# One stored table of cosines and sines per batch, read twice, with the sign taken in the scan

## The chip, the cores and the metric

The kernel runs on one core of a Trainium2 chip. The core has a matrix engine (TensorE, in the profile PE, with its weight loads as PEld), a vector engine (VectorE, DVE), a scalar engine (ScalarE, ACT), a general engine (GpSimd, POOL) and an engine that issues transfers (SyncE, SP). Transfers run on the core's 16 DMA engines. The metric is device time of one execution in microseconds (us).

## The reference

One layer of a decoder with x of 1024 rows and 1024 columns, in float32:

```python
h = modulate(rms_norm(x, ffn1_norm), sh1, sc1)
x = x + 0.5 * g1 * swiglu(h, ffn1_w_gate, ffn1_w_up, ffn1_w_down)

h = modulate(rms_norm(x, mix_norm), sh2, sc2)
b_gate, c_gate, v, u = split(h @ w_in, [512, 1024, 1536])
y_conv = b_gate * causal_conv3(c_gate * v, conv_w)
y_ssm = s5_mixer(u, ...)
y_mix = concat([rms_norm(y_conv, out_norm_conv), rms_norm(y_ssm, out_norm_ssm)])
x = x + g2 * (y_mix @ w_out)

h = modulate(rms_norm(x, ffn2_norm), sh3, sc3)
x = x + 0.5 * g3 * swiglu(h, ffn2_w_gate, ffn2_w_up, ffn2_w_down)
return rms_norm(x, final_norm)
```

The part that the change touches is `s5_mixer`, a diagonal state space model of 32 groups, each with 16 channels and 64 complex states:

```python
lam_bar = exp(lam * dt)                       # a complex factor per group and state
bu      = einsum('gpc,bsgc->bsgp', b_bar, u)  # inputs of the states
state_t = lam_bar * state_(t-1) + bu_t        # over the 1024 rows
y       = Re(einsum('gcp,bsgp->bsgc', c, state)) + d_skip * u
y       = gelu(y);  y = y * sigmoid(y @ glu_w + glu_b)
```

## The kernel before, in words

The large products (two feed-forward networks of 2816 inner columns, the input projection, the output projection, the gate matrix) are cut into products of 128 by 128 by 512 on TensorE; most go through a seven-product scheme (`seven`), which forms sums of blocks on DVE and ACT and spares one product in eight. Weights are streamed: SP loads a raw chunk of 128 by 1024, POOL's queue may add a second one to it in memory (line 175), DVE and ACT turn it into the operands `w`. Three raw chunks may be held at a time. Side work is cut into steps by generators and put between the steps of the large products; a counter (`clock.after(n, ...)`) sets at which step of the products a piece of other work is put out. The order thus made is the program order on each engine.

The state space model stands in two places.

**Tables** (`ssm_batch(b)`, side work during the first feed-forward network, between about 225 and 430 us). The 32 groups are taken in 8 batches of 4. For each batch DVE and TensorE build the small matrices of the scan over blocks of 8 rows: `mk` (within a block), `mi` (inputs of a block to its state) and `mo` (state to outputs). They also build `rot`, 128 by 512, whose rows 0 to 63 are the cosines and rows 64 to 127 the sines of the angle by which each of 64 states has turned at each of 128 blocks, for 4 groups. All of them are stored to scratch memory (`mi_d`, `mk_d`, `mo_d`, `co_d`, `si_d`), since the room is needed for other things until the scan. `rot` is stored as two tables of 128 rows: `co_d` holds the cosines twice, `si_d` the sines and below them their negation, which ACT writes to `rott`. These work tiles share one tag, `bt`, with four buffers. A new tile of that tag must wait until the tile four before it is done with, a store that reads it included; the first tiles of a batch are those of `cmul`, whose products form `bb`, and DVE's queue stands while they wait. The last two stores of a batch are `mk_d` (four, 64 KB each) and `mi_d`, one store of 256 KB whose target is put as counts of 8, 16 and 512.

**Scan** (about 745 to 880 us, between the matrix products of the projections). The batches follow each other every 18 steps of the counter; a batch has five steps, at the steps 0, 2, 7, 10 and 17 of its own:

- `state_in`: TensorE multiplies u by `mi` (into `px`, 128 rows: 64 real parts, 64 imaginary parts) and by `mk` (into `py`).
- `state_turn`: DVE turns `px` back by the angle, so that the scan has a real factor only: `sX = co * px`, and `swx`, the product of `si` with the opposite half of `px`, one instruction for each half; then their sum.
- `state_scan`: DVE's scan along the 128 blocks, one for each group.
- `state_back`: the turn forward again: `swz` from `si` and the opposite half of `sX`, `co * sX`, and their sum, which is written over `co`.
- `outputs`: TensorE multiplies the states by `mo` on top of `py`, ACT applies gelu, SP stores the result.

The tables of the scan are loaded by `ld`, one SP transfer into a tile of 128 by 512 each. `mi`, `mk` and `mo` have one buffer, `u`, `co` and `si` two. At the start come mi, mk and mo of batch 0, then u, si and co of batches 0 and 1. Then, each some steps after the last reader: `mi`, `mk` of b+1 and `u` of b+2 (3 steps after `state_in(b)`), `si` of b+2 (5 after `state_back(b)`), `mo` of b+1 and `co` of b+2 (3 after `outputs(b)`). Rows of u reach memory by the stores `u_d` and come back, in another layout, as `ub`.

Of the kernel before, what the change touches and what calls it, by code (L numbers as in the profile page):

```python
# [13 lines left out]
F32 = mybir.dt.float32  # L14
F32R = mybir.dt.float32r
I32 = mybir.dt.int32
AF = mybir.ActivationFunctionType
ALU = mybir.AluOpType
# [3 lines left out]
P = 128  # L22
# [20 lines left out]
NB = 8  # L43
GB = G // NB
# [187 lines left out]
def hymba_layer(ctx: ExitStack, tc, x_d, xt_d, wm1_d, wmod_d, gu1_d, gs1_d, ds10_d, ds11_d, wl1_d, win_d, wcvb_d, wout_d, glu_d, gu2_d, gs2_d, wd2_d, ds20_d, ds21_d, ds22_d, wl2_d, cols_d, cond_d, lam_d, bc_d, out_d):  # L232
    nc = tc.nc
    V, A, T, SP = (InOrder(tc, e) for e in (nc.vector, nc.scalar, nc.tensor, nc.sync))

    def pool(name, bufs=1, **kw):
        return ctx.enter_context(tc.tile_pool(name=name, bufs=bufs, **kw))
# [5 lines left out]
    scratch = pool("scratch", space=DRAM)  # L243
# [789 lines left out]

    mi_d = scratch.tile([NB, P, GB * P], F32, name="mi_d")
    mo_d = scratch.tile([NB, P, GB * P], F32, name="mo_d")
    co_d = scratch.tile([NB, P, GB * P], F32, name="co_d")
    si_d = scratch.tile([NB, P, GB * P], F32, name="si_d")
    u_d = [scratch.tile([P, S], F32, name=f"u{i}_d") for i in range(4)]
    y_d = [scratch.tile([TAU, CH, 8, J], F32, name=f"y{i}_d") for i in range(4)]
    r8 = const.tile([P, G], F32, name="r8")  # L1040
# [165 lines left out]
    def ssm_batch(b):  # L1206
# [9 lines left out]
        def bt(name):  # L1216
            return bp.tile([P, 576], F32, tag="bt", name=name, bufs=4)
# [28 lines left out]
        r, t = bt(f"rot{b}"), bt(f"rott{b}")  # L1246
# [12 lines left out]
        tp = sm([P, 512], f"tp{b}")  # L1259
        for g in range(GB):  # L1260
            T.transpose(tp[:, g * P : (g + 1) * P], bl[:, g * P : (g + 1) * P], ident[:])
        A.activation(t[64:128, :512], r[64:128, :512], AF.Copy, scale=-1.0)
        for half in (slice(0, 64), slice(64, 128)):
            SP.dma_start(co_d[b, half], r[0:64, :512])
        SP.dma_start(si_d[b, 0:64], r[64:128, :512])
        SP.dma_start(si_d[b, 64:128], t[64:128, :512])
        yield
        kc = bt(f"kc{b}")
        kc3 = kc[:CH, :512].rearrange("p (g m) -> p g m", g=GB)
# [4 lines left out]
        for g in range(GB):  # L1274
            V.scalar_tensor_tensor(
                out=kc3[:, g, 0:CH], in0=ident[:CH, :CH], scalar=ssm["lam"][:CH, 3, b * GB + g : b * GB + g + 1], in1=kc3[:, g, 0:CH], op0=ALU.mult, op1=ALU.add
# [43 lines left out]
    def side1():  # L1320
        yield from combos1()
        clock.period = 4.5
        sb = side_open.enter_context(tc.tile_pool(name="sb", bufs=1, side="right"))
        with tc.tile_pool(name="sb1", bufs=1, side="right") as sb1:
            yield from ssm_base(sb, sb1)
        clock.period = BATCH_PERIOD
        bps.append(side_open.enter_context(tc.tile_pool(name="bp", bufs=1, side="right")))
        mod_home.pool = side_open.enter_context(tc.tile_pool(name="wmp", bufs=1, side="right"))
        share[0] = MODS[1]
        prm_load(0)  # L1330
        for _ in range(2):
            mod_fetch(mod_home)
        yield
        InOrder.strict = True
        for b in range(NB):
            for i, _ in enumerate(ssm_batch(b)):
                yield
                if i % 4 == 1:
                    yield from gate1()
        InOrder.strict = False  # L1340
# [216 lines left out]
    held = {}  # L1557

    def ld(tag, src, b, bufs=1):
        t = sp.tile([P, GB * P], F32, tag=tag, name=f"{tag}{b}", bufs=bufs)  # L1560
        SP.dma_start(t[:], src)
        return t
# [12 lines left out]
        SP.dma_start(held["u", b][:], u_groups(b))  # L1575

    def co_load(b):
        held["co", b] = ld("co", co_d[b], b, 2)

    def si_load(b):  # L1580
        held["si", b] = ld("si", si_d[b], b, 2)

    def in_loads(b):
        held["mi", b] = ld("mi", mi_d[b], b)
# [5 lines left out]
    LOW, HIGH = slice(0, 64), slice(64, 128)  # L1590
# [17 lines left out]
    def state_turn(b):  # L1608

        co, si, px = held["co", b], held["si", b], held.pop(("px", b))  # L1610
        X = held["X", b] = sp.tile([P, GB * J], F32, tag="sX", name=f"sX{b}")
        sw = sp.tile([P, GB * J], F32, tag="sw", name=f"swx{b}")
        V.tensor_tensor(out=X[:], in0=co[:], in1=px[:], op=ALU.mult)
        for to, of in ((LOW, HIGH), (HIGH, LOW)):
            V.tensor_tensor(out=sw[to], in0=si[to], in1=px[of], op=ALU.mult)
        V.tensor_tensor(out=X[:], in0=X[:], in1=sw[:], op=ALU.add)

    def state_scan(b):
# [8 lines left out]
    def state_back(b):  # L1627

        co, si, X = held["co", b], held.pop(("si", b)), held.pop(("X", b))
        sw = sp.tile([P, GB * J], F32, tag="sw", name=f"swz{b}")  # L1630
        for to, of in ((LOW, HIGH), (HIGH, LOW)):
            V.tensor_tensor(out=sw[to], in0=X[of], in1=si[of], op=ALU.mult)
        V.tensor_tensor(out=co[:], in0=X[:], in1=co[:], op=ALU.mult)
        V.tensor_tensor(out=co[:], in0=co[:], in1=sw[:], op=ALU.add)
        if b + 2 < NB:
            clock.after(5, lambda: si_load(b + 2))

    def outputs(b):
        st, py, mo = (held.pop((n, b)) for n in ("co", "py", "mo"))
        for g in range(GB):  # L1640
            late, early = slice(g * P + 1, (g + 1) * P), slice(g * P, (g + 1) * P - 1)
            T.matmul(py[:, late], lhsT=mo[:, g * P : (g + 1) * P], rhs=st[:, early], start=False, stop=True, skip_group_check=True)
        yg = sp.tile([P, GB * J], F32, tag="yg", name=f"yg{b}")
        A.activation(yg[:], py[:], AF.Gelu_apprx_tanh)
        SP.dma_start(y_groups(b), yg[:].rearrange("p (g j) -> p g j", g=GB))
        if b + 1 < NB:
            clock.after(3, lambda: mo_load(b + 1))
        if b + 2 < NB:
            clock.after(3, lambda: co_load(b + 2))
# [3 lines left out]
    for b in range(2):  # L1653
        u_load(b)
        si_load(b)
        co_load(b)
# [6 lines left out]
    def split_g(h):  # L1663
        actG[h] = []
        for i in range(4):
            clock.after(2 * i, lambda i=i, h=h: actG[h].append(split_act(yb[i][:, hsl(h)], f"yg{i}_{h}")))

    STEPS = (0, state_in), (2, state_turn), (7, state_scan), (10, state_back), (17, outputs)
    for b in range(NB):
        for n, step in STEPS:  # L1670
# [307 lines left out]
```

## Time and profile before

| | |
|---|---|
| median of 3 runs | 1679.19 us (1677.68 to 1680.28) |
| profiled execution, its own time | 1679.18 us |
| its span (first to last instruction) | 1677.3 us |
| mean granted TensorE clock | 0.989 |
| PE busy | 1642.3 us (98%) |
| DVE busy | 1142.2 us (68%) |
| ACT busy | 723.3 us (43%) |
| moved by DMA | 348.44 MB, 208 GB/s over the span |
| stores of a table half: co_d<-rot, si_d<-rot, si_d<-rott | 16, 8 and 8, of 128 KB each |
| loads of a table: co<-co_d, si<-si_d | 8 and 8, of 256 KB each |
| the negation, rott<-rot on ACT | 8 of 627 ns |

All times of the profile are of the one profiled execution. "SPq" and "POOLq" name the transfers that SP and POOL issue; a row of such a queue tells how long the issue took, and the view of DMA issues how long it took from there to the landing. In a row of the timeline the brackets hold the time for which the engine stood idle before the instruction, and what ended it. In the view by stretches the DMA column is the mean busy share of the 16 DMA engines, and the clock that of TensorE.

### The profile page before, as it was taken

What the parts mean: (1) busy time and instruction counts of PE and PEld (TensorE: products, weight loads), DVE (VectorE), ACT (ScalarE), POOL (GpSimd) and SP (SyncE); (2) the same over time, 40 slices, a digit from 0 to 9 for tenths busy, and PEclk for the clock granted to TensorE, in tenths of its full rate; (3) what the DMA queues carried; (4) which work ended last, traced back from release to release, by engine and by line L of the source; (5) the groups of instructions that cost most, each with busy time, mean ns of one, the idle gap of its engine ahead of it and who ended that gap; (6) DMA issues with size and microseconds to landing.
All of it is one profiled execution on the core that took longest, in us unless ns stands there. A gap on an engine that the chain in (4) does not pass through costs nothing.

```text
span 1677.3 us, 20625 instructions
## 1 busy us (share of the span) xinstructions
PE 1642.3 (98%) x7437; PEld 1353.9 (81%) x7437; DVE 1142.2 (68%) x1699; ACT 723.3 (43%) x1072; POOL 182.3 (11%) x223
## 2 busy tenths in 40 slices
PE   8999999999999999999997999999999999999997
PEld 5888888878878888788886788888888888888887
DVE  6984487868576768798885868856555655444576
ACT  6654333333454442463232447444444444322345
POOL 2010100000100102200000022000001001000104
PEclk9999999999999999999998999999999999999999
DMA  9466789988987766668857313558877877889832
GB/s 349 142 165 171 194 250 265 270 242 248 267 249 202 199 226 198 216 186 232 218 149 249 113 44 142 137 140 224 239 226 205 222 219 223 282 267 324 244 72 100
DMA packets 132023, 348.44 MB, mean 208 GB/s; under 512 B 16977, under 2 KB 40785, under 8 KB 130898
## 3 DMA queue, kind: packets, MB, share of 16 engines
q1 hardware_dynamic: 113490, 281.07, 47.4%
q0 software_dynamic: 18432, 66.07, 23.1%
q8 instruction: 58, 0.95, 0.2%
q14 instruction: 43, 0.35, 0.1%
HBM read 261.75 MB, written 76.94 MB: 202 GB/s over the span
## 4 chain that ended last, share of the span: by engine, by line
PE 69%; DVE 5%; DMA 3%; issue 1%; ACT 1%; POOL 1%; SPq 0%; DVEq 0%; POOLq 0%; ACTq 0%
PE wo L113 5%; PE fald L113 4%; PE fbd_1B L113 3%; PE fbd_0B L113 3%; PE fad_1B L113 2%; PE fad_0B L113 2%; PE u L113 2%; PE fbd_1C L113 1%; PE fbd_0C L113 1%; PE gl L113 1%; PE fad_1C L113 1%; PE fad_0C L113 1%; PE fb10d L113 1%; DVE w L113 1%; PE fb0d L113 1%
## 5 line engine op out<-in xcount | busy, mean ns | idle before, releaser
L113 DVE TENSOR_TENSOR w<-raw,w 128x1024 fp32r<-128x1024 f32 (+1 forms) x256 | 308.8, 1207 | 238.2 <-ACT w L113 237.2
L113 ACT CAST w<-raw 128x1024 fp32r<-128x1024 f32 (+1 forms) x256 | 266.0, 1040 | 300.5 <-DMA raw<-in_ds 59.3
L175 POOL DMA_DIRECT2D raw<-in_gs x80 | 70.4, 883 | 740.2 <-DVE w L113 445.5
L113 DVE CUSTOM_DVE_ANT_0 wm<-wm,cact 128x1024 f32<-128x1024 f32 x56 | 72.3, 1308 | 1.3 <-DMA wm<-in_wmod 1.2
L175 POOL DMA_DIRECT2D raw<-in_ds x36 | 31.5, 875 | 312.2 <-DVE w L113 201.4
L113 PE MATMUL wo<-oa,w 128*128 128x512 f32 x192 | 50.7, 427 | 6.8 <-DVE oa L113 3.5
L113 PEld LDWEIGHTS wo<-oa,w 128*128 128x128 f32 x192 | 39.7, 209 | 16.9 <-DVE oa L113 4.7
L113 PE MATMUL p<-h,w 128*128 128x512 f32 x192 | 49.4, 407 | 1.8 <-ACT h L113 1.5
L113 PE MATMUL wo<-ob,w 128*128 128x512 f32 x192 | 44.8, 391 | 0.0
L113 PE MATMUL u<-h,w 128*128 128x512 f32 x192 | 44.5, 391 | 0.0
L113 PEld LDWEIGHTS p<-h,w 128*128 128x128 f32 x192 | 35.7, 192 | 10.0 <-ACT h L113 2.0
L113 PEld LDWEIGHTS u<-h,w 128*128 128x128 f32 x192 | 35.8, 188 | 7.7 <-DVE h L113 0.4
L113 PEld LDWEIGHTS wo<-ob,w 128*128 128x128 f32 x192 | 35.7, 188 | 7.3
L175 POOL DMA_DIRECT2D raw<-in_wcvb x12 | 10.5, 879 | 141.7 <-DVE w L113 88.6
L113 ACT COPY wa<-wo 128x512 f32<-128x512 f32 x16 | 9.4, 589 | 37.5 <-PE wo L113 36.6
L113 PE MATMUL fb0u<-h,w 128*128 128x512 f32 x96 | 23.8, 391 | 0.0
L113 PE MATMUL fb0g<-h,w 128*128 128x512 f32 x96 | 23.2, 389 | 0.0
L113 PE MATMUL fald<-fa9lA,w 128*128 128x512 f32 x96 | 22.8, 391 | 0.0
L113 PE MATMUL gl<-yg,w 128*128 128x512 f32 x96 | 22.7, 391 | 0.0
L113 PE MATMUL fald<-fa0lA,w 128*128 128x512 f32 x96 | 22.4, 389 | 0.0
L113 PE MATMUL fald<-fa10lA,w 128*128 128x512 f32 x96 | 22.4, 389 | 0.0
L113 PEld LDWEIGHTS fb0g<-h,w 128*128 128x128 f32 x96 | 18.0, 188 | 3.8
(1662 smaller groups left out, 4059.5 us busy)
## 6 DMA issues: line engine op xcount, KB each, us to landing
raw<-in_gs SPq DMA_DIRECT2D x80, 512.0 KB, 5.5
raw<-in_gs POOLq DMA_DIRECT2D x80, 512.0 KB, 6.5
wm<-in_wmod SPq DMA_DIRECT2D x56, 512.0 KB, 6.3
raw<-in_ds SPq DMA_DIRECT2D x32, 512.0 KB, 5.0
raw<-in_ds POOLq DMA_DIRECT2D x32, 512.0 KB, 7.0
mw<-in_wm SPq DMA_DIRECT2D x8, 1024.0 KB, 13.5
raw<-in_wcvb SPq DMA_DIRECT2D x12, 512.0 KB, 4.1
raw<-in_wcvb POOLq DMA_DIRECT2D x12, 512.0 KB, 6.8
```

The costliest lines, as they stand in the source:

```text
L113: r = getattr(self.engine, name)(*args, **kw)
L175: self.G.dma_start(out=r, in_=src, accum_op=ALU.add)
```

## The change

The cosines and sines of a batch, which lie below each other in one tile of 128 rows, go to memory in one store, `cs_d[b]`, as two tables of 64 rows. The four stores of half tables and the negated copy by ACT are gone. Each of the two loads now has a half table as its source, repeated by a leading dimension with step 0, so that the 64 rows arrive in both halves of the tile: `co` holds the cosines twice as before, `si` now the sines twice, without the sign. The sign is put into the product in which the negated half was used: in `state_turn` that of the high half, in `state_back` that of the low half, where `scalar_tensor_tensor` multiplies by −1 and by the sine in one instruction. The tile of `swz` so gets the same values as before.

```diff
--- before.py
+++ after.py
@@ -1033,8 +1033,7 @@
 
     mi_d = scratch.tile([NB, P, GB * P], F32, name="mi_d")
     mo_d = scratch.tile([NB, P, GB * P], F32, name="mo_d")
-    co_d = scratch.tile([NB, P, GB * P], F32, name="co_d")
-    si_d = scratch.tile([NB, P, GB * P], F32, name="si_d")
+    cs_d = scratch.tile([NB, 2, 64, GB * P], F32, name="cs_d")
     u_d = [scratch.tile([P, S], F32, name=f"u{i}_d") for i in range(4)]
     y_d = [scratch.tile([TAU, CH, 8, J], F32, name=f"y{i}_d") for i in range(4)]
     r8 = const.tile([P, G], F32, name="r8")
@@ -1259,11 +1258,7 @@
         tp = sm([P, 512], f"tp{b}")
         for g in range(GB):
             T.transpose(tp[:, g * P : (g + 1) * P], bl[:, g * P : (g + 1) * P], ident[:])
-        A.activation(t[64:128, :512], r[64:128, :512], AF.Copy, scale=-1.0)
-        for half in (slice(0, 64), slice(64, 128)):
-            SP.dma_start(co_d[b, half], r[0:64, :512])
-        SP.dma_start(si_d[b, 0:64], r[64:128, :512])
-        SP.dma_start(si_d[b, 64:128], t[64:128, :512])
+        SP.dma_start(cs_d[b].rearrange("a p m -> (a p) m"), r[:, :512])
         yield
         kc = bt(f"kc{b}")
         kc3 = kc[:CH, :512].rearrange("p (g m) -> p g m", g=GB)
@@ -1575,10 +1570,10 @@
         SP.dma_start(held["u", b][:], u_groups(b))
 
     def co_load(b):
-        held["co", b] = ld("co", co_d[b], b, 2)
+        held["co", b] = ld("co", cs_d[b, 0].unsqueeze(0).to_broadcast([2, 64, GB * P]), b, 2)
 
     def si_load(b):
-        held["si", b] = ld("si", si_d[b], b, 2)
+        held["si", b] = ld("si", cs_d[b, 1].unsqueeze(0).to_broadcast([2, 64, GB * P]), b, 2)
 
     def in_loads(b):
         held["mi", b] = ld("mi", mi_d[b], b)
@@ -1611,8 +1606,8 @@
         X = held["X", b] = sp.tile([P, GB * J], F32, tag="sX", name=f"sX{b}")
         sw = sp.tile([P, GB * J], F32, tag="sw", name=f"swx{b}")
         V.tensor_tensor(out=X[:], in0=co[:], in1=px[:], op=ALU.mult)
-        for to, of in ((LOW, HIGH), (HIGH, LOW)):
-            V.tensor_tensor(out=sw[to], in0=si[to], in1=px[of], op=ALU.mult)
+        V.tensor_tensor(out=sw[LOW], in0=si[LOW], in1=px[HIGH], op=ALU.mult)
+        V.scalar_tensor_tensor(out=sw[HIGH], in0=px[LOW], scalar=-1.0, in1=si[HIGH], op0=ALU.mult, op1=ALU.mult)
         V.tensor_tensor(out=X[:], in0=X[:], in1=sw[:], op=ALU.add)
 
     def state_scan(b):
@@ -1628,8 +1623,8 @@
 
         co, si, X = held["co", b], held.pop(("si", b)), held.pop(("X", b))
         sw = sp.tile([P, GB * J], F32, tag="sw", name=f"swz{b}")
-        for to, of in ((LOW, HIGH), (HIGH, LOW)):
-            V.tensor_tensor(out=sw[to], in0=X[of], in1=si[of], op=ALU.mult)
+        V.scalar_tensor_tensor(out=sw[LOW], in0=X[HIGH], scalar=-1.0, in1=si[HIGH], op0=ALU.mult, op1=ALU.mult)
+        V.tensor_tensor(out=sw[HIGH], in0=X[LOW], in1=si[LOW], op=ALU.mult)
         V.tensor_tensor(out=co[:], in0=X[:], in1=co[:], op=ALU.mult)
         V.tensor_tensor(out=co[:], in0=co[:], in1=sw[:], op=ALU.add)
         if b + 2 < NB:
```

On DVE 16 of the 64 by 512 products become the form with a scalar; its number of instructions is the same. ACT has 8 instructions fewer, SP 24 transfers fewer (three for each batch). The order of the instructions on TensorE and POOL is the same.

The first place is SP's order in the table building, the end of a batch: `wm` is a chunk of the modulation's matrix, `kept4Y` to `kept4W` are stores of the feed-forward network. Before:

```order
L113 DMA wm_2_0_1948<-in_wmod 128x1024
L113 DMA co_d<-rot_1913 64x512 x2
L113 DMA si_d<-rot_1913 64x512
L113 DMA si_d<-rott_1914 64x512
L113 DMA kept4Y<-fa4Y 128x1024
L113 DMA kept4Z<-fa4Z 128x1024
L113 DMA kept4W<-fa4W 128x1024
L113 DMA mk_d<-kc_1979 16x8x128 x4
L113 DMA mi_d<-mi_1981 8x16x512
```

And with the change:

```order
L113 DMA wm_2_0_1947<-in_wmod 128x1024
L113 DMA cs_d<-rot_1912 128x512
L113 DMA kept4Y<-fa4Y 128x1024
L113 DMA kept4Z<-fa4Z 128x1024
L113 DMA kept4W<-fa4W 128x1024
L113 DMA mk_d<-kc_1974 16x8x128 x4
L113 DMA mi_d<-mi_1976 8x16x512
```

One store of 128 rows stands where four of 64 stood; what follows is in the same order.

The second place is SP's order at the start of the scan: the first loads of the tables (two of each), then the stores and loads of u. Before:

```order
L113 DMA mk_6055<-mk_d 128x4x128
L113 DMA mo_6057<-mo_d 128x512
L113 DMA si_6061<-si_d 128x512
L113 DMA co_6063<-co_d 128x512
L113 DMA si_6067<-si_d 128x512
L113 DMA co_6069<-co_d 128x512
L113 DMA u_d<-ya_5666 128x1024
L113 DMA u_d<-ya_5667 128x1024
L113 DMA ub_6059<-u_d 128x4x128
L113 DMA ub_6065<-u_d 128x4x128
```

And with the change:

```order
L113 DMA mk_6022<-mk_d 128x4x128
L113 DMA mo_6024<-mo_d 128x512
L113 DMA si_6028<-cs_d 128x1x512
L113 DMA co_6030<-cs_d 128x1x512
L113 DMA si_6034<-cs_d 128x1x512
L113 DMA co_6036<-cs_d 128x1x512
L113 DMA u_d<-ya_5633 128x1024
L113 DMA u_d<-ya_5634 128x1024
L113 DMA ub_6026<-u_d 128x4x128
L113 DMA ub_6032<-u_d 128x4x128
```

Nothing has moved; the four loads of co and si have another source. The row shows the tile's side; on the source's side the counts are 2 (step 0), 64 and 512, where they were 128 and 512.

The third place is SP's order at the end of the first network's inner part, around 440 to 485 us, where the order of loads follows the counter: `x_0`, `x_1` are rows of x, `raw` a chunk of the second matrix, `fa1lS` to `fa4lS` kept operands. Before:

```order
L113 DMA x_0_3569<-in_x 128x1024
L113 DMA raw_3712<-in_ds 128x1024
...
L113 DMA raw_3763<-in_ds 128x1024
...
L113 DMA x_0_3571<-in_x 128x1024
L113 DMA raw_3813<-in_ds 128x1024
L113 DMA x_1_3573<-in_x 128x1024
L113 DMA x_1_3575<-in_x 128x1024
```

And with the change:

```order
L113 DMA x_0_3536<-in_x 128x1024
L113 DMA x_0_3538<-in_x 128x1024
L113 DMA raw_3679<-in_ds 128x1024
...
L113 DMA x_1_3540<-in_x 128x1024
L113 DMA raw_3730<-in_ds 128x1024
...
L113 DMA raw_3780<-in_ds 128x1024
L113 DMA x_1_3542<-in_x 128x1024
```

Two of the loads of x stand one or two chunks of the matrix further ahead.

## The prediction

> **What bounds the kernel now.** I read the page first. TensorE is busy through the whole span:
>
> ```profile
> PE 1642.3 (98%) x7437; PEld 1353.9 (81%) x7437; DVE 1142.2 (68%) x1699; ACT 723.3 (43%) x1072; POOL 182.3 (11%) x223
> ```
>
> 35 us of the 1677.3 us span are left in which PE does nothing (1677.3 − 1642.3). So taking work from DVE, ACT or a queue can win only a part of those 35 us, while anything that makes PE wait is paid in full. I then looked at the two stages that the change touches: the scan (about 726 to 880 us), in which the tables are read, and the table building (about 225 to 430 us). The stretches of the scan, one for each of its batches, come from the view of busy time by stretch; the columns are length, PE, PEld, DVE, ACT, POOL, granted clock, mean busy share of the 16 DMA engines, GB/s:
>
> ```profile
> 726.00:738.00 12.00, 12.00 (x54) 9.94 (x54) 12.00 (x21) 7.21 (x14) 0.00 (x0) 1.00 0.40 134
> ...
> 751.00:766.00 15.00, 15.00 (x81) 12.87 (x80) 11.19 (x19) 6.16 (x8) 0.86 (x1) 1.00 0.95 282
> 766.00:782.00 16.00, 16.00 (x88) 13.79 (x86) 13.30 (x20) 4.31 (x6) 2.62 (x3) 1.00 0.93 244
> 782.00:797.00 15.00, 15.00 (x80) 12.87 (x79) 14.84 (x24) 3.89 (x5) 0.00 (x0) 1.00 0.75 194
> 797.00:813.00 16.00, 16.00 (x83) 13.42 (x82) 14.76 (x24) 3.78 (x5) 0.86 (x1) 1.00 0.70 175
> 813.00:827.00 14.00, 14.00 (x75) 12.01 (x75) 9.86 (x16) 5.30 (x7) 1.72 (x2) 1.00 0.96 264
> 827.00:843.00 16.00, 15.28 (x80) 12.80 (x79) 15.78 (x25) 3.29 (x4) 0.86 (x1) 1.00 0.71 202
> ```
>
> PE is without a gap there, and that rests on DMA engines that are already busy 70 to 96% of the time, and on a VectorE nearly as full. There is hardly any idle DMA time in which a slower transfer could lie.
>
> **Part 1, the loads of the scan.** Before, each of the 8 batches reads 256 KB of cosines and 256 KB of sines, 128 rows on both sides. Now each read has the same size, but its source is a half table of 64 rows taken twice: source counts 2, 64, 512 (the first with step 0). The trace of before has no such load. The nearest row is the one store whose slowest dimension is not a multiple of 16: mi_d, written with an outer count of 8 from a tile of 128 rows. The last one before 348 us is seen nearly alone, since SP issues nothing more until 353 us and POOL nothing until 351 us:
>
> ```profile
> 344.33 0.63 SPq L113 DMA_DIRECT2D mi_d<-mi  x1
> 353.24 0.35 SPq L113 DMA_DIRECT2D wm<-in_wmod  x1
> ```
>
> and POOL's next transfer:
>
> ```profile
> 351.21 0.89 POOL L175 DMA_DIRECT2D raw<-in_gs  x1 [12.09 <-DVE w L113]
> ```
>
> The busy time of that half microsecond, and of four with full queues:
>
> ```profile
> 347.50:348.00 0.50, 0.50 (x4) 0.35 (x2) 0.47 (x3) 0.00 (x0) 0.00 (x0) 1.00 0.51 176
> 450.00:454.00 4.00, 4.00 (x19) 3.34 (x18) 2.52 (x3) 2.90 (x5) 0.00 (x0) 1.00 1.04 412
> ```
>
> In its tail half of the engines are busy (0.51 of 16 is 8), where transfers of 128 rows fill all (1.04). I read from it that the outer count sets how many engines share a transfer: 8 gives 8 engines, 128 gives 16, and the new loads, with 2, get **two engines**. That is an inference from one count to another, and the largest risk of this prediction.
>
> The Trainium skill, "DMA: Bandwidth & Descriptors", section "Why a DMA increments its semaphore by 16 and not by 1", says the same as a rule: the number of engines is the largest one up to 16 that divides the slowest dimension above 1 on both sides, and the lowest-numbered engines are taken. Its section "Rules for kernel authors" names this very form, a leading zero-stride broadcast of c copies, as confined to c engines, so the page speaks against the change; the 0.51 agrees with it for a count of 8, and no run yet shows a count of 2. By the page the sum is that of the forecast; without it, rival A.
>
> The rate of one engine: 412 GB/s over 16 × 1.04 is 24.8 GB/s; 176 over 16 × 0.51 is 21.6. On two engines each carries 131,072 bytes: 5.3 us at 24.8 (taken, since these loads move rows of 2 KB like the big transfers), 6.1 at 21.6. On 16 engines the share of one is 16,384 bytes, 0.66 us. So a load adds 5.3 − 0.66 = 4.6 us to two engines (up to 5.4), and a batch, with two, **9.3 us** (up to 10.8). The other fourteen get freer, which helps nobody: every transfer of 128 rows also needs its piece from the two slow ones, and behind them on the same SP queue.
>
> *Start of the scan.* Four such loads are issued within 2 us, and the rows of u follow them (the queue's rows, then PE's):
>
> ```profile
> 725.62 0.49 SPq L113 DMA_DIRECT2D si<-si_d  x1
> 726.15 0.43 SPq L113 DMA_DIRECT2D co<-co_d  x1
> 726.62 0.43 SPq L113 DMA_DIRECT2D si<-si_d  x1
> 727.10 0.43 SPq L113 DMA_DIRECT2D co<-co_d  x1
> 738.43 3.31 SPq L113 DMA_DIRECT2D u_d<-ya  x2
> 741.83 1.30 SPq L113 DMA_DIRECT2D ub<-u_d  x2
> ...
> 751.42 0.44 SPq L113 DMA_DIRECT2D mi<-mi_d  x1
> ...
> 752.42 0.61 SPq L113 DMA_DIRECT2D mk<-mk_d  x1
> ```
>
> ```profile
> 749.86 1.05 PE L113 MATMUL px<-ub,mi 128*128 128x128 f32 x8
> ...
> 764.80 1.05 PE L113 MATMUL px<-ub,mi 128*128 128x128 f32 x8
> 765.69 1.06 PE L113 MATMUL py<-ub,mk 128*128 128x128 f32 x8
> ```
>
> On the two engines the four take 4 × 5.3 = 21.2 us; the other transfers of 726 to 738 take 0.40 × 12 − 4 × 0.66 = 2.2 us. So they are free near 749, not 729. The store u_d of 738.43 passes them only then (about 751), its load ub is issued after it has landed, and lands some 4 to 5 us later, near 756. PE's px, which takes ub, ran at 749.86: PE stands for about **6 us** (4 if the queues share kindly, 12 if the second u_d and the first weights get between). Behind px on PE stand py and all projection matmuls; DVE's sX waits for px.
>
> *The six stretches.* Their DMA shares times lengths are 14.25 + 14.88 + 11.25 + 11.20 + 13.44 + 11.36 = 76.4 us of busy time per engine in 92 us. Each holds two table loads (batches 2 to 7): 6 × 9.3 = 55.8 us more on the two engines, 132.2 in all, which is 40 us more than there is. A part of it the prefetch covers once: mi and mk are asked for at 751.42 and 752.42 and used at 764.80 and 765.69, 13.3 us later. The view of DMA issues (KB each, median us to landing) gives the landings from 726 to 858 us, 3.6 for mi:
>
> ```profile
> si<-si_d SPq DMA_DIRECT2D x8, 256.0 KB, 3.7
> co<-co_d SPq DMA_DIRECT2D x8, 256.0 KB, 5.1
> ...
> mi<-mi_d SPq DMA_DIRECT2D x7, 256.0 KB, 3.6
> ```
>
> With some 4 us for both that leaves a slack of 9 us, used up in the first two batches. mi and mk have one buffer, so the next are asked for only after px and py of the batch; from then on each batch takes as long as its two engines need, about 5 us more than PE. Sum **+31 us** (40 − 9). Bounds: +16, if the two buffers of co and si lend another batch of 15 us; +48, at 21.6 GB/s (6 × 10.8 = 65 in place of 55.8) without any slack.
>
> **Part 2, the tables.** One store of 128 rows takes the place of three 64-row stores and a fourth with its negation. In before the next batch's first DVE products waited for one of them, and PE felt it twice. The landings of the stores issued from 334 to 348 us, the wait on DVE, the two on PE, and the clock behind the second:
>
> ```profile
> co_d<-rot SPq DMA_DIRECT2D x2, 128.0 KB, 9.9
> ...
> si_d<-rot SPq DMA_DIRECT2D x1, 128.0 KB, 10.3
> ```
>
> ```profile
> 347.38 0.49 DVE L113 TENSOR_TENSOR bb<-prm,qq 128x128 f32<-128x128 f32 x2 [8.36 <-DMA si_d<-rot]
> ```
>
> ```profile
> 348.92 3.02 PE L113 MATMUL fa7uB<-h,w 128*128 128x512 f32 x12 [0.60 <-DVE fa7uc L113]
> 364.84 1.86 PE L113 MATMUL kp<-cl,bl 128*16 128x128 f32 x8 [3.39 <-DVE bl L113]
> ```
>
> ```profile
> 366.00:370.00 4.00, 4.00 (x14) 3.04 (x13) 2.78 (x4) 1.68 (x3) 0.00 (x0) 0.50 1.03 305
> ```
>
> The sines were the third store in that queue and landed 10.3 us after their issue at 336.9, so at 347.2; the new store stands first and has the bytes of the two cosine stores, which landed 9.9 us after 335.7, at 345.6: **1.6 us sooner**. I take 0.6 + 1.6 of the two gaps, and 0.8 of the clock of 0.50 behind the second: **−3 us**. Bounds: 0, if what is late next (the rest of blt and the mi_d and mk_d stores, which hold the same four buffers) keeps DVE as long; −6, if both gaps go (3.99) and with them the half clock of the four us behind (2.0). Other batches stop no PE at this point.
>
> **Part 3, what costs nothing.** ACT loses eight negations, SP 24 issues; DVE takes 16 products in another form. The negation's row, and DVE's groups in the scan (busy us, mean ns):
>
> ```profile
> L113 ACT ACTIVATE rott<-rot x8: 627/627/631, 227.3 to 421.1; 64x512 f32<-64x512 f32 x8
> ```
>
> ```profile
> L113 DVE TENSOR_TENSOR swx<-si,px 64x512 f32<-64x512 f32 x16 | 11.0, 687 | 0.2
> ...
> L113 DVE SCALAR_TENSOR_TENSOR ya<-buu,ya 128x512 f32<-128x512 f32 x1 | 0.7, 691 | 0.0
> ```
>
> ACT's 5 us lie beside PE (ACT is 43% busy), and SP's issues with them. The form with a scalar takes 691 ns where the plain one takes 687: 16 × 0.004 is 0.06 us, and even on DVE's path it is nothing. The loads of x that move one or two places ahead in SP's order before the second half of the first FFN stand beside an existing wait there (in brackets, idle time and its releaser):
>
> ```profile
> 484.71 0.50 PE L113 MATMUL fad_0C<-fa1lS,w 128*128 128x512 f32 x1 [1.70 <-DVE w L113]
> ```
>
> Weights a load later could lengthen it by one load's time (+3), or the order could remove it (−1.7); I take 0.
>
> **Sum**: 1679.2 (the profiled execution, whose span is 1677.3; the median is 1679.19, the same) + 6 + 31 − 3 = **1713 us**. Its own range: 4 + 16 − 6 − 1.7 gives 1691, 12 + 48 + 0 + 3 gives 1742.
>
> **Rivals.**
>
> *A, the loads keep 16 engines* (15%). mi_d has its count of 8 on the side of the memory it writes; the new count of 2 stands on the side that is read, and the tile has 128 rows. If only the tile's side decides, landings stay at 3.7 and 5.1 us, the stage is as before, and part 2 alone is left: 1676, between 1673 and 1679. For it: the trace has no transfer with a small count on the source. Against it: mi_d's tile too had 128 rows and did not get 16. It decides from more than about eight engines on: with eight a load takes 1.3 us per engine and a batch 1.3 us more, which the free 5 to 30% of the stretches hold. This is the case on the other side: faster, if the gain is above 3.4 us.
>
> *B, two engines, but the queue of work drains* (8%). If successive loads fell on different pairs, or the weights' own waits left the two engines room, the 55.8 us would spread and only the start were left: 1679.2 + 4 to 12 − 3, some 1680 to 1688. Against it: four loads and two u_d follow each other without a gap, and the stage's busy share leaves 16 us of 92.
>
> *C, weights starve as well* (3%). Each matrix chunk has a load and an accumulating one behind it; with a full ring on two engines, each of these is late by a table load, PE stops for weights between the batches and its clock falls as at 366 us. Sixty us and more, above 1745.
>
> **How the numbers follow.** The forecast has 74%, most of it between 1691 and 1742. I extend the range down to 1680 to take in B, and up to 1745; left out are A and C, under 2 in 10. A change under 0.2% (3.4 us) cannot be told from none by this measurement. Faster by more: 9% of A's 15. Within: 6% from A and 1% from B, 7%. Slower: 74 + 7 + 3 = 84%.
>
> **What would show it.** Right: the loads of co and si land after more than 8 us each; in the scan PE waits for DMA of ub, mk or mi, or for DVE co behind them; PE's idle time in the stretches rises from 0.7 us (16.00 − 15.28) to 30 or more, and the mean DMA share over the stretches falls while they get longer. In the table stage the wait of bb shrinks by 1 to 2 us. Wrong: landings as before and PE without gaps in the scan (A); one gap near 750 and none after it (B). The step to doubt first is the count of engines, the next one the slack of 9 us.

## The result, and the profile after

The changed kernel takes 1700.99 us (median of 4 runs, 1698.81 to 1703.52) where the kernel before, run beside it, takes 1678.64 us: a ratio of 1.0133 (95% interval 1.0117 to 1.0148), 22 us slower. Its profiled execution took 1700.51 us, with a span of 1698.4 us. The kernel before was run again beside every set of runs below, and its median stayed between 1678.15 and 1678.64 us, so medians of different sets are subtracted from each other in what follows.

The page of the changed kernel, its row of busy times:

```profile
PE 1647.9 (97%) x7437; PEld 1357.4 (80%) x7437; DVE 1142.0 (67%) x1699; ACT 718.0 (42%) x1064; POOL 182.4 (11%) x223
```

The span grew by 21.1 us. Of these, 5.6 are PE's busy time: its instructions are the same 7437, so this is products at a lower clock. The other 15.5 are idle time of PE (50.5 in place of 35.0). The new waits stand in one place and are longer than that, since some waits ahead of the scan went away. The groups of PE's products in the scan (726 to 880 us; busy us, mean ns, idle time before them and its releasers):

```profile
L113 PE MATMUL py<-ub,mk 128*128 128x128 f32 x64 | 11.1, 331 | 0.5 <-DMA mk<-mk_d 0.5
L113 PE MATMUL px<-ub,mi 128*128 128x128 f32 x64 | 10.7, 319 | 20.3 <-DMA mi<-mi_d 11.9 <-DMA ub<-u_d 8.4
```

In the timeline of the changed kernel these are one wait at the start of the scan and four later ones:

```profile
750.68 2.05 PE L113 MATMUL px<-ub,mi 128*128 128x128 f32 x8 [8.44 <-DMA ub<-u_d]
...
801.62 1.16 PE L113 MATMUL px<-ub,mi 128*128 128x128 f32 x8 [3.51 <-DMA mi<-mi_d]
...
821.72 1.13 PE L113 MATMUL px<-ub,mi 128*128 128x128 f32 x8 [2.53 <-DMA mi<-mi_d]
...
841.91 2.04 PE L113 MATMUL px<-ub,mi 128*128 128x128 f32 x8 [4.98 <-DMA mi<-mi_d]
...
877.57 1.13 PE L113 MATMUL px<-ub,mi 128*128 128x128 f32 x8 [0.86 <-DMA mi<-mi_d]
```

From these rows and those of before the whole difference can be laid out. PE comes to its first px at 750.68 − 8.44 = 742.24, where it was 749.86: 7.6 us won ahead of the scan. The first wait takes 8.4 back. From the first to the last px, before 749.86 to 856.68 (106.8 us), it now takes 750.68 to 877.57 (126.9 us): 20.1 lost. −7.6 + 8.4 + 20.1 is 20.9 of the 21.1 us. DVE shows no wait on a load of co or si in the scan: what comes late is ub and mi, which stand behind these loads in the queue.

How many engines the new loads use can be read directly from two stretches behind the four first loads, in which the other DMA engines stand still (columns as in the stretches of before: the last three are clock, DMA share, GB/s):

```profile
727.00:733.00 6.00, 6.00 (x28) 4.96 (x27) 6.00 (x11) 4.80 (x9) 0.00 (x0) 1.00 0.13 51
743.00:748.00 5.00, 0.00 (x0) 0.00 (x0) 1.09 (x1) 0.31 (x1) 0.00 (x0) 0.74 0.13 46
```

0.13 of 16 engines is 2.1, and 51 GB/s over two engines is 25.5 GB/s each. Between the two, from 733 to 741 us, the stores u_d and weights move and the share is 0.98; what is left after that runs on two engines again. In the second stretch PE does nothing at all. SP's own queue shows the same jam, in the changed kernel:

```profile
717.84 0.59 SPq L113 DMA_DIRECT2D si<-cs_d  x1
718.48 0.53 SPq L113 DMA_DIRECT2D co<-cs_d  x1
719.06 3.71 SPq L113 DMA_DIRECT2D si<-cs_d  x1
722.81 5.00 SPq L113 DMA_DIRECT2D co<-cs_d  x1
730.65 3.32 SPq L113 DMA_DIRECT2D u_d<-ya  x2
747.86 0.92 SPq L113 DMA_DIRECT2D ub<-u_d  x2
```

The third and fourth loads take 3.71 and 5.00 us to issue alone, where 0.43 to 0.49 was normal, and ub, which needs the store u_d to have landed, goes out 17.2 us behind it; before it was 3.4 us (738.43 to 741.83).

Behind a long wait PE is also slower. Five stretches of the changed kernel:

```profile
748.00:752.00 4.00, 1.32 (x6) 1.35 (x7) 0.00 (x0) 0.00 (x0) 0.00 (x0) 0.50 0.78 245
752.00:756.00 4.00, 4.00 (x17) 3.64 (x17) 3.14 (x6) 0.00 (x0) 0.00 (x0) 0.55 0.98 340
...
801.00:805.00 4.00, 2.90 (x17) 2.74 (x18) 2.15 (x5) 0.00 (x0) 0.00 (x0) 0.80 0.69 211
...
821.00:825.00 4.00, 3.28 (x23) 3.05 (x24) 2.06 (x3) 0.00 (x0) 0.00 (x0) 1.00 0.89 275
...
841.00:845.00 4.00, 3.09 (x14) 3.12 (x15) 1.00 (x2) 0.00 (x0) 0.00 (x0) 0.50 1.03 231
```

Behind the waits of 8.44 and 4.98 us the granted clock is a half, and px takes 2.05 us in place of 1.05. Behind the one of 3.51 us px still takes 1.16, and the clock falls after it (the py that follows takes 1.94 in place of 1.06). Behind the one of 2.53 us it stays at 1.00. The Trainium skill, "TensorE: Matmul & The Clock Gate", section "HAM oscillation — how this bites in real kernels", asks for no idle gaps of PE above some 3.4 us, as the clock falls behind them; the rows of this kernel agree, with the fall between 2.53 and 3.51 us. The length of the wait alone does not settle it: a wait of 2.97 us in experiment 7 was followed by a clock of 0.63 (364 to 368 us), one of 3.38 in experiment 6 by 1.00.

In the table stage the waits of before got smaller, in the changed kernel's timelines of SP's queue, DVE and PE:

```profile
333.34 0.42 SPq L113 DMA_DIRECT2D cs_d<-rot  x1
```

```profile
343.39 0.29 DVE L113 TENSOR_TENSOR bb<-prm,qq 128x128 f32<-128x128 f32 x1 [4.99 <-DMA cs_d<-rot]
```

```profile
360.65 1.03 PE L113 MATMUL kp<-cl,bl 128*16 128x128 f32 x8 [0.63 <-DVE bl L113]
```

bb starts at 343.4 in place of 347.4, and PE waits 0.63 us in place of 3.39, with no wait at fa7uB and no fall of the clock. The clock is the largest part: in before it was 0.50 from 364 to 370 us and 0.92 from 370 to 374, which is 3.3 us lost, and in the changed kernel it was 1.00 from 360 on. With 2.8 us at kp and 0.6 at fa7uB that makes 6.7. The whole gain is there when PE leaves the stage: fa9uA, a product behind the last batch, starts at 423.8 in place of 430.7 us, 6.9 sooner, and that is ahead of the loads of x whose order changed.

### The profile page after: what moved, and what is told of

Its sections match the earlier page's. It is cut to its first block, busy times and chain, and to the rows that moved or that the text cites. A ratio compares the mean times of both kernels' runs of the same rounds, so it can differ in the third digit from the quotient of the medians.

```text
span 1698.4 us, 20554 instructions
## 1 busy us (share of the span) xinstructions
PE 1647.9 (97%) x7437; PEld 1357.4 (80%) x7437; DVE 1142.0 (67%) x1699; ACT 718.0 (42%) x1064; POOL 182.4 (11%) x223
## 4 chain that ended last, share of the span: by engine, by line
PE 84%; DMA 7%; DVE 4%; ACT 2%; issue 1%; POOL 1%; SPq 0%; POOLq 0%; DVEq 0%; ACTq 0%
PE wo L113 5%; PE fald L113 3%; PE fbd_1B L113 3%; PE fbd_0B L113 3%; PE p L113 3%; PE fad_0B L113 2%; PE fad_1B L113 2%; DMA mi<-mi_d 2%; PE fbd_1C L113 1%; PE fbd_0C L113 1%; PE u L113 1%; PE gl L113 1%; PE fad_0C L113 1%; PE fad_1C L113 1%; PE fb10d L113 1%
## 5 line engine op out<-in xcount | busy, mean ns | idle before, releaser
L113 PE MATMUL px<-ub,mi 128*128 128x128 f32 x64 | 10.7, 319 | 20.3 <-DMA mi<-mi_d 11.9
L113 PEld LDWEIGHTS px<-ub,mi 128*128 128x128 f32 x64 | 9.6, 225 | 22.6 <-issue 14.2
L113 DVE TENSOR_TENSOR sX<-co,px 128x512 f32<-128x512 f32 x8 | 5.5, 686 | 26.1 <-PE px L113 26.1
```

Source lines behind the costliest of these rows:

```text
L113: r = getattr(self.engine, name)(*args, **kw)
```

## The experiments

All of them are built on the changed kernel or on the one before; ratios are to the kernel before, run beside them, with the 95% interval.

**1. Loads of 64 rows on both sides.** Is it the form of the load?

```diff
-        held["co", b] = ld("co", cs_d[b, 0].unsqueeze(0).to_broadcast([2, 64, GB * P]), b, 2)
+        held["co", b] = ld2("co", cs_d[b, 0], b)
...
+    def ld2(tag, src, b):
+        t = sp.tile([P, GB * P], F32, tag=tag, name=f"{tag}{b}", bufs=2)
+        for half in (slice(0, 64), slice(64, 128)):
+            SP.dma_start(t[half], src)
+        return t
```

(and the same for si).

> The changed kernel, but each table load is two loads of 64 rows (64 on both sides) in place of one with a leading count of 2; store, sign and all else as in the change. Two-engine theory: the 128 rows are spread over 16 engines again, every wait of PE on ub and mi in the scan goes, and only the gain ahead of the scan is left (PE reached its first px 7.6 us sooner than before, 742.24 against 749.86): 1671 us, landings of si and co back at 3 to 6 us. Rival (reading the same 64 rows twice is what is slow, whatever the form): the waits stay, 1690 to 1701 us. Rival (the loss is in DVE's new form of the products): 1700 us.

Measured: 1671.45 us, ratio 0.9951 (0.9932 to 0.997). The landings in its view of DMA issues, and PE's waits from 716 to 870 us, which are all that is left there:

```profile
si<-cs_d SPq DMA_DIRECT2D x16, 128.0 KB, 4.6
co<-cs_d SPq DMA_DIRECT2D x16, 128.0 KB, 5.4
```

```profile
PE py L113 <- DVE co L113: 1.5, 2, 0.8
```

The form of the load is the loss, the whole of it: 1700.99 − 1671.45 = 29.5 us. From the first to the last px the profiled execution takes 107.0 us, as before the change (106.8), so that the same rows are read twice costs nothing there, nor does DVE's new form. This version is faster than both kernels, than the one before by 0.5%.

**2. Only the first four loads in the broadcast form**, the rest as in 1.

```diff
-        held["co", b] = ld("co", cs_d[b, 0].unsqueeze(0).to_broadcast([2, 64, GB * P]), b, 2)
+        if b < 2:
+            held["co", b] = ld("co", cs_d[b, 0].unsqueeze(0).to_broadcast([2, 64, GB * P]), b, 2)
+        else:
+            held["co", b] = ld2("co", cs_d[b, 0], b)
```

(and the same for si).

> The changed kernel, but only the tables of the batches 0 and 1, loaded at the start of the scan, come in the form with the leading count of 2; those of batches 2 to 7 come as two loads of 64 rows. Theory of two additive terms (start, and overload of the two engines later): the wait of px on ub near 750 stays at about 8 us and all later ones go, so 1671 + 9 = 1680 us. Rival (the start's delay is what all later waits follow from, since each load is asked for one batch ahead): later waits of 10 us and more remain, 1690 us or more.

Measured: 1682.47 us, ratio 1.0021 (1.001 to 1.0033). PE's waits from 716 to 880 us:

```profile
PE px L113 <- DMA ub<-u_d: 8.2, 1, 8.2
PE py L113 <- DVE co L113: 1.5, 2, 0.8
```

One wait, and no later one follows from it. The start costs 1682.5 − 1671.5 = 11.0 us, the wait of 8.2 and about 3 us of lower clock behind it (0.50 from 748 to 752 us, 0.74 from 752 to 756).

**3. The reverse: only the loads of batches 2 to 7 in the broadcast form** (`b >= 2` in the condition of 2).

> The reverse of the run with the broadcast form at the start alone: batches 0 and 1 as two loads of 64 rows each, batches 2 to 7 with the leading count of 2. If the two terms add: 1701.0 - 11.0 (1682.5 against 1671.5) = 1690 us, no wait near 740, and waits on mi from about the third batch on. If the first stall lent the later loads time: the later waits grow by up to its 8 us, 1698 us. If the late state of the start is what makes the later loads late: 1675 us or less.

Measured: 1692.1 us, ratio 1.0085 (1.0069 to 1.0101). PE's waits from 716 to 880 us:

```profile
PE px L113 <- DMA mi<-mi_d: 9.3, 5, 4.1
PE py L113 <- DMA mk<-mk_d: 3.5, 2, 3.1
PE py L113 <- DVE co L113: 1.3, 2, 0.7
```

The later loads cost 1692.1 − 1671.5 = 20.6 us, without any late start. With the 11.0 of experiment 2 that is 31.6, against 29.5 for both together: the two terms add, within what these runs can tell.

**4. Only co in the broadcast form**, si as in 1: half the bytes on the two engines.

> The changed kernel, but only co comes in the form with the leading count of 2, si as two loads of 64 rows: half the bytes on the two engines. Overload theory (a threshold: the two engines have some room, and the loss begins where it is used up): at the start two loads are 10.6 us and done near 730, so no wait on ub; later 4.6 us more per batch against a free share of some 15 us in six stretches plus 9 us of slack, so 0 to 5 us of waits: 1671 to 1677 us. Proportional theory (each two-engine load costs the same): half of 29 us, 1685 us.

Measured: 1673.41 us, ratio 0.9967 (0.9951 to 0.9983). PE's waits from 716 to 870 us:

```profile
PE py L113 <- DVE co L113: 1.4, 2, 0.7
PE px L113 <- DMA mi<-mi_d: 0.3, 1, 0.3
```

Half of the loads cost some 2 us (1673.4 − 1671.5), within the spread of these runs, not half of 29.5; from the first to the last px the profiled execution takes 107.4 us against 107.0 with half loads. The loss begins at a threshold: two engines had room for one table in each batch and not for two.

**5. mi and mk asked for a batch sooner.** Are they only behind a late co in the queue, or is there no capacity?

```diff
-        held["mi", b] = ld("mi", mi_d[b], b)
-        held["mk", b] = ld("mk", mk_d[b], b)
+        held["mi", b] = ld("mi", mi_d[b], b, 2)
+        held["mk", b] = ld("mk", mk_d[b], b, 2)
...
-        if b + 1 < NB:
-            clock.after(3, lambda: in_loads(b + 1))
+        if b + 2 < NB:
+            clock.after(3, lambda: in_loads(b + 2))
...
     in_loads(0)
+    in_loads(1)
```

> The changed kernel with its two-engine loads, but mi and mk have two buffers and are asked for one batch sooner (those of batch 1 at the start, ahead of the four table loads). Overload theory (the two engines cannot move the bytes in the time): one more batch of slack, about 13 us, is used up once, the wait near 750 stays, so 1687 to 1692 us. Latency theory (mi is merely behind one late co in the queue): the later waits on mi go and only the start is left, 1680 us. If the waits are of the tables themselves: 1701 us.

Measured: 1697.01 us (1693.83 to 1703.62, the profiled one being the slowest), ratio 1.0108 (1.0078 to 1.0137). PE's waits from 726 to 890 us:

```profile
PE px L113 <- issue: 10.5, 1, 10.5
PE py L113 <- DMA mo<-mo_d: 5.7, 2, 3.6
PE py L113 <- DVE co L113: 2.9, 2, 2.6
PE cv2gB L113 <- DVE cv2gc L113: 2.0, 1, 2.0
...
```

No wait on mi is left, and most of the time is still lost: the waits have gone to mo, which still has one buffer, and to co. The first wait is longer, 10.5, with two more loads ahead of it; the profile names no releaser for it, but ub goes out at 749.76 us and px starts at 752.76, some 3 us later, as in the changed kernel. 4 us were won where the overload theory allowed 9 to 14 and the latency theory wanted 21. It speaks for want of capacity, without showing it; the size of the slack it was to measure is not settled by it, since mo took the place.

**6. A count of 4.** Does the count of the slowest dimension set the number of engines, or only a step of 0? The scratch table gets gaps, so that the slowest dimension of a load's source can't be merged with the next.

```diff
-    cs_d = scratch.tile([NB, 2, 64, GB * P], F32, name="cs_d")
+    cs_d = scratch.tile([NB, 2, 4, 16 * GB * P + GB * P], F32, name="cs_d")
...
-        SP.dma_start(cs_d[b].rearrange("a p m -> (a p) m"), r[:, :512])
+        SP.dma_start(cs_d[b].rearrange("a k w -> (a k) w")[:, :16 * GB * P].rearrange("k (r m) -> k r m", r=16), r[:, :512])
...
+        for half in (slice(0, 64), slice(64, 128)):
+            SP.dma_start(t[half], cs_d[b, i, :, :16 * GB * P].rearrange("k (r m) -> k r m", r=16))
```

> Two loads for each table as above, but the scratch table has gaps, so that the slowest dimension of each load's source counts 4 (16 rows each) while the tile's side has 64 rows; the store's counts 8. If the smaller count of the two sides sets the number of engines: in the stretch with nothing else in flight the share is 0.25, four engines, a batch adds 4.0 us to them (5.3 against 1.3), the same as the co-only run, and the time is 1672 to 1679 us. If any count below 16 falls to one or two engines: 1695 us or more. If only a step of 0 does it: as with half loads, shares near 1, 1671 us.

Measured: 1674.64 us (1670.08 to 1680.7), ratio 0.9983 (0.9966 to 1.0). Its stretch with the first loads alone, and PE's waits from 716 to 870 us:

```profile
724.50:731.50 7.00, 7.00 (x32) 5.79 (x32) 7.00 (x13) 3.95 (x7) 0.00 (x0) 1.00 0.26 100
```

```profile
PE py L113 <- DVE co L113: 1.5, 2, 0.8
```

0.26 of 16 is 4.2: four engines, with no step of 0 in the load. So 2, 4 and 8 give 2, 4 and 8 (0.13, 0.26, and 0.51 for mi_d), whether the memory with the small count is read, as here, or written, as in mi_d; a small count on the tile's side and a step of 0 with a larger count were not tried. The scan has no wait on a load, and takes 107.0 us from the first to the last px, as with half loads. Four engines are enough, with a margin that was not measured.

The median is 3.2 us above that of experiment 1, and that stands ahead of the scan: PE comes to its first px at 744.7 us, in experiment 1 at 739.9. The one store of a batch has a leading count of 8 here, as mi_d has, and gaps in memory. The waits of bb in the table stage, PE's wait at kp and the start of fa9uA:

```profile
DVE bb L113 <- DMA cs_d<-rot: 24.8, 6, 8.8
```

```profile
364.46 1.03 PE L113 MATMUL kp<-cl,bl 128*16 128x128 f32 x8 [3.38 <-DVE bl L113]
...
427.57 2.88 PE L113 MATMUL fa9uA<-h,w 128*128 128x512 f32 x12
```

The wait at kp is that of before (3.39), only without the fall of the clock behind it, and fa9uA comes 3.1 us sooner than in before where the changed kernel gains 6.9.

**7. The change without its stores**: those of before and the negation kept, the two loads in the broadcast form from the first 64 rows of `co_d` and `si_d`, the sign in the scan.

```diff
-        held["co", b] = ld("co", co_d[b], b, 2)
+        held["co", b] = ld("co", co_d[b, 0:64].unsqueeze(0).to_broadcast([2, 64, GB * P]), b, 2)
...
-        held["si", b] = ld("si", si_d[b], b, 2)
+        held["si", b] = ld("si", si_d[b, 0:64].unsqueeze(0).to_broadcast([2, 64, GB * P]), b, 2)
```

> The kernel before with its stores and the negation kept, but the loads in the form with the leading count of 2 (from the first 64 rows of co_d and of si_d) and the sign in the scan. If the two parts add: 1678.2 + 29.5 (1701.0 of the change against 1671.5 with half loads) = 1708 us, with waits of PE in the scan alone. If part of the loss comes only because the scan starts 8 us sooner than its loads are due: less, 1700 us.

Measured: 1704.73 us, ratio 1.0159 (1.0138 to 1.018), 26.4 us more than before. PE's waits from 716 to 890 us:

```profile
PE px L113 <- DMA mi<-mi_d: 12.7, 4, 4.9
PE px L113 <- DMA ub<-u_d: 8.8, 1, 8.8
```

The same waits as in the changed kernel (11.9 and 8.4), on a scan that starts as late as before (PE comes to its first px at 750.6 us, before at 749.9). The time lies between the two that were expected: the two parts add to within some 3 us.

**8. The sign alone**: the kernel before, without the negation, the sines stored twice from `rot`, the sign in the scan.

```diff
-        A.activation(t[64:128, :512], r[64:128, :512], AF.Copy, scale=-1.0)
...
-        SP.dma_start(si_d[b, 64:128], t[64:128, :512])
+        SP.dma_start(si_d[b, 64:128], r[64:128, :512])
```

> The kernel before with the sign alone moved: no negation on ACT, all four 64-row stores kept (the sines now stored twice from rot), the loads as before, the scan's products as in the change. If the gain ahead of the scan comes from fewer bytes and stores that stand ahead of the next batch's first products: no change, 1677 to 1680 us, and bb still waits some 17 us in all. If it comes from the negation that no longer holds rott and its store back: 1671 to 1673 us. If the new form of the products costs DVE's path anything: above 1680 us.

Measured: 1679.36 us, ratio 1.001 (0.9999 to 1.002): no difference. PE's two waits in the table stage are there as before:

```profile
348.73 3.03 PE L113 MATMUL fa7uB<-h,w 128*128 128x512 f32 x12 [0.79 <-DVE fa7uc L113]
364.65 1.86 PE L113 MATMUL kp<-cl,bl 128*16 128x128 f32 x8 [3.37 <-DVE bl L113]
```

fa9uA starts at 430.4 us, before at 430.7. So the gain of the table stage comes neither from ACT nor from the form of the products; what is left of the change ahead of fa9uA is the stores.

**9 and 10. What of the stores?** Both on the version of experiment 1. In 9 the merged store goes out twice, the second time to memory that nobody reads (the bytes of before). In 10 it is cut into four stores of 32 rows (the issues of before).

```diff
         SP.dma_start(cs_d[b].rearrange("a p m -> (a p) m"), r[:, :512])
+        SP.dma_start(cx_d[b].rearrange("a p m -> (a p) m"), r[:, :512])
```

> The version with two 64-row loads for each table (1671.5 us), but the table of 128 rows is stored a second time, to memory that nobody reads, so that 512 KB for each batch are stored as before, in two issues in place of four and without the negation. If the bytes that bb must wait for make the gain: the wait of bb is back at 15 us or more and PE waits near 350 to 365 us, 1676 to 1679 us. If the negation or the number of stores makes it: 1671 to 1673 us.

```diff
-        SP.dma_start(cs_d[b].rearrange("a p m -> (a p) m"), r[:, :512])
+        cs = cs_d[b].rearrange("a p m -> (a p) m")
+        for q in range(0, P, 32):
+            SP.dma_start(cs[q : q + 32], r[q : q + 32, :512])
```

> The version with two 64-row loads for each table (1671.5 us), but the merged store is cut into four stores of 32 rows (64 KB each): the bytes of the change, the number of issues of before, no negation. If the number of stores on SP's queue made the late landings: the longest wait of bb is back at 8 us, PE waits near 350 and 365 us, 1676 to 1679 us. If it was the sum of bytes and issues or the form with 64 rows: 1671 to 1673 us.

Measured: 1673.12 us, ratio 0.9974 (0.996 to 0.9988), and 1672.39 us, ratio 0.9971 (0.9955 to 0.9987). Neither the bytes alone nor the number of issues alone takes the gain away. The waits of bb in the table stage, twice stored and then in four stores (in all, times, longest):

```profile
DVE bb L113 <- DMA cx_d<-rot: 17.4, 6, 5.0
```

```profile
DVE bb L113 <- DMA cs_d<-rot: 17.1, 5, 4.8
```

In before it is 17.3 us in 5, with a longest of 8.4. These waits move from one execution to the next: in the changed kernel and in experiments 1 to 4, whose table stage is the same, they are 6.3 to 15.0 us in all and the longest 3.2 to 5.8. So the sums settle nothing; that the longest stays below 8.4 holds in all of them, and PE's wait at kp is then 1.5 us at most.

The start of fa9uA tells more. It comes at 422.7 to 424.7 us in the changed kernel and experiments 1 to 5, and here too, at 423.3 and 423.9. In before and experiment 8 it comes at 430.7 and 430.4; in experiment 7, which has the stores of before, at 428.1. Experiment 6 stands close to these, with 427.6 and a longest wait of bb of 8.8, though it has one store for each batch and half the bytes of before. So neither fewer bytes nor fewer issues is needed by itself, and both together are not enough: with a leading count of 8 (and gaps) the single store loses about half of the gain. Why the four stores of 64 rows, which have no small count, are late as well stays open, and each of these figures is of one profiled execution.

## Why the prediction was right, and where it was off

The direction, the place and the mechanism were right: 1713 was forecast, 1701 came, in a range of 1680 to 1745. The steps were less exact than the total. By its steps:

- *Count 8 gives 8 engines, so count 2 gives two.* Right, and now measured: shares of 0.13 and 51 GB/s. It was an inference from one store; experiment 6 adds a count of 4. Rival A (16 engines, 15%) falls with it. Its threshold, "more than about eight engines", was too careful: four are enough (experiment 6).
- *24.8 GB/s for one engine, 5.3 us for a load.* Measured 25.5 GB/s, which makes 5.1 us.
- *The start, +6 us (4 to 12).* The wait came where it was forecast, at px behind ub, with 8.4 us, and cost 11.0 (experiment 2). What the step left out is the clock: the table stage was priced with it, the scan was not. The loads also started 8 us sooner, with the scan. The forecast had ub issued at about 751 us for want of the two engines; with loads 7.8 us earlier that is 743, and it went out at 747.86, some 5 us later than the step's sum; px then followed 2.8 us after the issue, where 4 to 5 were taken for the landing. The two misses partly offset each other.
- *The six stretches, +31 us (16 to 48).* This is the term that was mis-sized: 20.6 (experiment 3). The loss without a late start (experiment 3) and its threshold (experiment 4) are shown. That the two engines want capacity, and mi is not merely behind late loads, is what experiment 5 speaks for without showing it. The sum was 40 less a slack of 9 us; the threshold runs fit a slack of about 20 as well: with co alone 6 × 4.6 is 27.6 us more on 76.4, or 104 in 92, 12 over, and nothing was lost to speak of. The step's upper bound was added up wrongly by 1 us: 76.4 + 65 − 92 is 49, not 48. What the runs do not separate is whether the slack was greater or the busy share of 76.4 us counted more than what the two engines could not do at the same time.
- *Which wait comes last.* Forecast were ub, mk or mi, or co: ub and mi it was, mk with 0.5 us.
- *The tables, −3 us (0 to −6).* Outside its own range: 6.7 by time (1678.15 − 1671.45; 5.0 to 11.4 by the interval, the sign and the reordering in it), and 7.6 in the profile up to the scan. The largest error is the clock: 0.8 us were taken for it and 2.0 allowed, from the four us behind the wait; the fall of before lasted from 364 to beyond 370 and cost 3.3. bb came 4.0 us sooner in place of 1.6 (at 343.4, though in experiment 1, with the same stage, at 338.4). The forecast took over the time of the issue from before; the batches ahead of this one had gained too, and the store went out at 333.3 in place of 335.7.
- *The order of the loads of x, 0 (−1.7 to +3).* The existing wait of 1.70 us at fad_0C is gone in the changed kernel and in experiment 1, and still there, with 1.51, in experiment 8. The changed kernel has one of 0.9 at fad_0B instead, and in experiment 10 1.3 us at fad_0C came back. So at most the 1.7 of the range were won, and the order alone was not tried.
- *The sign, 0.* Right: ratio 1.001 (0.9999 to 1.002).
- *The signs of being right.* The mean DMA share fell, from 0.84 (750 to 857 us) to 0.66 (750 to 878). PE's idle time in the scan rose to 22 us and not to the 30 that were named, which is the error of the six stretches again. The landings of co and si can't be held against the 8 us that were named: the view gives none for them.
- *Rivals B and C.* In B only the start would be left; that is experiment 2's kernel, not this one. For C weights would have to starve; PE has no wait on a weight in the scan.

That the total came so near is in part luck: the start was 5.0 us too low (+6 for +11.0), the six stretches 10.4 too high (+31 for +20.6), so half of the larger error was made good by the smaller one. The error of the tables, 3.7 us (−3 for −6.7), goes the same way as that of the six stretches. 34 was forecast, 25 is the sum of the measured terms (11.0 + 20.6 − 6.7), and 22 was measured.

## What to carry to other kernels

Before a load is given a broadcast source or any other new shape, look at the count of the slowest dimension on each side and compare it with the 16 DMA engines: here 2 made two engines carry all, and the same bytes as two loads of 64 rows kept the share between 0.74 and 1.04 while the first of them ran (716 to 722 us in experiment 1). The average DMA share hides such a load: over the scan it fell from 0.84 to 0.66 while PE waited for transfers, which looks like room to spare. So read the share in a stretch where the transfer is alone. Here the slow loads were paid by what landed behind them in the same queue with one buffer, or with a store ahead of it. Half of them cost some 2 us, all of them 29.5: a test with a part of the loads would have shown no harm.

Do the same for stores. The one store with a leading count of 8 in experiment 6 lost about half of what the merged store had won.

## What was not expected of the hardware

The issue itself took longer behind two such loads: SP needed 3.71 and 5.00 us for the third and the fourth, 0.59 and 0.53 for the first two, and 0.43 to 0.49 for each in before. With four engines, in experiment 6, none of the first four pairs of loads took more than 1.42 us. And the gain of the merged store survived both a doubling of its bytes and a cut into four, while about half of it went with a leading count of 8.
